# Keeping the split projection weights of a hybrid streaming encoder in HBM between blocks of rows

## The chip, the core and the metric

The kernel runs as one program on one core of a Trainium2 chip. The metric is device time in microseconds (us) of one execution; the time before is the median of three runs, 3382.91 us (3378.88 to 3388.88). The profile that is read below is one further execution, with the profiler on.

## The reference

Two layers work on 2048 prompt rows and 64 sample rows of width 1024. Cut to what matters here, one layer is:

```python
xn = rms(x, lp['norm_g'])                     # row norm, gain folded into the weights by the kernel
aq, ak, av, ag, bcq, bckv, bkr, bg, cq, ck, cv, cg, mq, mg = split_in(xn @ lp['w_in'])   # 1024 -> 3232
# four attention groups: A chunk band, B low-rank over the whole past, C stick-breaking, M memory
...
y = rms(heads(y, N_OUT_HEADS), lp['out_g'].reshape(N_OUT_HEADS, HEAD_DIM))
y = y.reshape(x.shape[:2] + (MIX_WIDTH,)) * jax.nn.silu(gates)
return x + y @ lp['w_out']                     # 1024 -> 1024
```

All of it is float32. A product of two float32 matrices is made of three matmuls of a rounded type: each factor is split into a high part and the rest (low part), and high x high, high x low and low x high are summed.

## The kernel before

**Tiles and blocks.** Rows are worked on in 17 tiles of 128 (16 of the prompt, one of the sample rows). Three blocks hold 6, 6 and 5 tiles; the sample tile is the last of the third. For each layer and block there is an input projection job (`i` in the order string of line 1366, then layer and block) and an output projection job (`o`); `m` is the projection of the memory tokens. The string sets the order of the jobs: `i00 m00 i01 i02 o00 m10 o01 i10 i11 o02 i12 o10 o11 o12`. So each layer's w_in is used by three jobs (its blocks 0, 1, 2, in that order), and so is its w_out.

**A job.** `p_stream` (line 326) walks a job's chunks of output columns: 13 for an input projection (12 of 256 columns, one of 160), 4 of 256 for an output projection. For each chunk it walks the block's tiles, and for each tile eight slices k of 128 input rows. A tile and a slice take three matmuls, lines 402 (high x high), 403 (high x low weights) and 405 (low activations x high); the sample tile leaves out line 405, and the narrow chunk joins 402 and 403 into line 400. Weights are the moving operand, so a chunk's eight slices stay in SBUF until the block's last tile is through.

**Weights.** `weights` (line 297) is a generator that `feed` (line 337) advances by two steps per tile, one chunk ahead of the matmuls. Of a chunk it loads four `raw` tiles (two slices each, 256 KB, 4 buffers, line 314), and for each slice makes a `wh` tile (2 KB per partition, 8 buffers) that holds the high part (line 304, GpSimd, gain folded in) beside the low part (line 305, VectorE). A `wh` buffer is free again when the last tile of the chunk before has used its slice.

**Beside it.** `attention` (line 1253) is a second stream of instructions: scores (855 to 858), softmax or stick-breaking (`s`, `cc`, `r`, lines 1026 to 1113), transposes (900), the split of the probabilities (903, 136) and the product with the values (925). Its loads are `qbuf`, `qr` (one buffer), `kv` (five), `bt` (one buffer, line 1176). A main loop (line 1448) takes turns between the two streams by a target curve of matmul costs, which does not count weight splits or loads. The framework then sets each engine's own order of instructions and hands out buffers by a simulation of the engines (line 1558, `schedule_with_timeline_sim=True`). Each engine runs its instructions in that order. All DMAs are issued by SyncE (SP), one after the other: one whose operand is not ready holds up all behind it.

Of the kernel before, what the change touches and what calls it, by code (L numbers as in the profile page):

```python
# [7 lines left out]
F32 = mybir.dt.float32  # L8
F32R = mybir.dt.float32r
# [9 lines left out]
COL = {}  # L19
# [45 lines left out]
def hybrid_step(  # L65
# [8 lines left out]
    nc = tc.nc  # L74
# [12 lines left out]
    def pool(name, bufs=1, **kw):  # L87
        return ctx.enter_context(tc.tile_pool(name=name, bufs=bufs, **kw))
# [4 lines left out]
    pj = pool("pj")  # L93
# [47 lines left out]
    def dt(name, shape, dtype=F32):  # L141
        return dram.tile(shape, dtype, name=name, tag=name)
# [3 lines left out]
    D = {}  # L146

    def layer_dram(l):
        d = {}
        for b, tl in enumerate(blocks):  # L150
            d["QR", b] = dt(f"qr{l}_{b}", [3, 128, len(tl) * 128])
            for g in "ABCM":
                d["Q" + g, b] = dt(f"q{g}{l}_{b}", [2, 256, len(tl) * 128])
                d["G" + g, b] = dt(f"g{g}{l}_{b}", [128, len(tl), 256])
        for g in "ABC":
            d["KV" + g] = dt(f"kv{g}{l}", [2, NH, HD, (NT + 3) // 4, 2, 512])
        for s in ("SA", "SB", "SC", "M", "SM"):
            d["KV" + s] = dt(f"kv{s}{l}", [2, NH, HD, 2, 256])
        d["KR"] = dt(f"kr{l}", [128, NT * 128])
        d["KRS"] = dt(f"krs{l}", [128, 256])  # L160
        d["Y"] = {t: dt(f"y{l}_{t}", [128, 1024]) for t in range(NT + 1)}
        D[l] = d

# [111 lines left out]
    class Job:  # L275
# [1 line left out]


        def __init__(self, tiles, loader, norm, wsrc, gcols, chunks, need=None, start=None, side=None, second=None,
                     sample=True):  # L280
            self.tiles, self.loader, self.norm = list(tiles), loader, norm
            self.wsrc, self.gcols, self.chunks = wsrc, gcols, chunks
            self.need, self.start, self.side, self.second = need, start, side, second
            self.need_fold = sample
            self.acts = {}
            for c in chunks:
                left[c[3]] = left.get(c[3], 0) + len(self.tiles)
# [8 lines left out]

    def weights(job, c0, w, out):

        gc = job.gcols()

        def split(raw, k):
            hl = pj.tile([128, 512], F32R, tag="wh", name="wh", bufs=8)
            h, lo = hl[:, 0:w], hl[:, w:2 * w]
            G.tensor_scalar(out=h, in0=raw, scalar1=gc[:, k:k + 1], scalar2=1.0, op0=ALU.mult, op1=ALU.mult)  # L304
            V.scalar_tensor_tensor(out=lo, in0=raw, scalar=gc[:, k:k + 1],  # L305
                                   in1=h.bitcast(F32), op0=ALU.mult, op1=ALU.subtract)
            out.append((hl[:, 0:2 * w], h, lo))

        n = 2
        src = job.wsrc[:, 8 * c0:8 * (c0 + w)].rearrange("p (k c) -> p k c", k=8)  # L310
        raws = []
        for k in range(0, 8, n):
            raw = pj.tile([128, n, 256], F32, tag="raw", name="raw", bufs=4)
            nc.sync.dma_start(out=raw[:, :, 0:w], in_=src[:, k:k + n])
            raws.append(raw)
            yield 0
            if k > 0:
                for i in range(n):
                    split(raws[-2][:, i, 0:w], k - n + i)
                    yield 0  # L320
        for i in range(n):
            if i:
                yield 0
            split(raws[-1][:, i, 0:w], 8 - n + i)
# [396 lines left out]
    def load_x(l):  # L721
        def loader(t):
            def f(x, q):
                cs = slice(q * 512, (q + 1) * 512)
                if l > 0 and t == SAMP:
                    for e in range(2):
                        nc.sync.dma_start(out=x[64 * e:64 * e + 64], in_=X1[t][0:64, cs])
                elif l > 0:
                    nc.sync.dma_start(out=x, in_=X1[t][:, cs])
                elif t == SAMP:  # L730
                    for e in range(2):
                        nc.sync.dma_start(out=x[64 * e:64 * e + 64], in_=x_sample[:, cs])
                else:
                    nc.sync.dma_start(out=x, in_=x_prompt[t * 128:(t + 1) * 128, cs])
            return f
        return loader

    def in_proj(l, b):
        def side():
            yield from caches(l)  # L740
            done.add(("caches", l))

        return Job(blocks[b], load_x(l), True, w_in[l], lambda: LC[l]["gc"][:, 0:8], chunk_fns(l, b),
                   need=("out", l - 1, b) if l > 0 else None,
                   start=lambda: layer_consts(l), side=side if b == 1 else None,
                   second=lambda: layer_weights(l))

    def mem_proj(l):
        d = D[l]
# [63 lines left out]
    def out_proj(l, b):  # L813
        d = D[l]

        def loader(t):
            def f(x, q):
                cs = slice(q * 512, (q + 1) * 512)
                if t == SAMP:
                    for e in range(2):  # L820
                        nc.sync.dma_start(out=x[64 * e:64 * e + 64], in_=d["Y"][t][0:64, cs])
                else:
                    nc.sync.dma_start(out=x, in_=d["Y"][t][:, cs])
            return f

        def fin(c):
            def fn(t, pp, rstd):
                xr = pj.tile([128, 256], F32, tag="ev", name="xr", bufs=3)
                cs = slice(c * 256, (c + 1) * 256)
                if l > 0:  # L830
                    nc.sync.dma_start(out=xr, in_=X1[t][:, cs])
                elif t == SAMP:
                    G.memset(xr, 0.0)
                    nc.sync.dma_start(out=xr[0:64], in_=x_sample[:, cs])
                else:
                    nc.sync.dma_start(out=xr, in_=x_prompt[t * 128:(t + 1) * 128, cs])
                yield
                V.tensor_tensor(out=xr, in0=pp, in1=xr, op=ALU.add)
                yield
                if l < L - 1:  # L840
                    nc.sync.dma_start(out=X1[t][:, cs], in_=xr)
                elif t == SAMP:
                    nc.sync.dma_start(out=y_s[:, cs], in_=xr[0:64])
                else:
                    nc.sync.dma_start(out=y_p[t * 128:(t + 1) * 128, cs], in_=xr)
            return fn

        return Job(blocks[b], loader, False, w_out[l], lambda: LC[l]["gc"][:, 16:24],
                   [(c * 256, 256, fin(c), ("out", l, b)) for c in range(4)], need=("attn", l, b))


    def scores(ps, q, qr, i, kt, kr, c0, n):
# [509 lines left out]
    for l in range(L):  # L1362
        layer_dram(l)
# [84 lines left out]
    while gens:  # L1448
# [12 lines left out]
        c = next(gens[s], "end")  # L1461
# [109 lines left out]
```

## Time and profile before

| what | value |
|---|---|
| median of 3 runs | 3382.91 us (3378.88 to 3388.88) |
| profiled execution, its own time | 3392.03 us |
| its span, first to last instruction | 3390.2 us |
| mean granted TensorE clock | 0.985 |
| matmuls / weight loads, busy | 94% / 89% |
| VectorE / ScalarE / GpSimd, busy | 80% / 57% / 47% |
| DMA engines, share of time on the kernel's own queue | 58.3% |
| HBM read / written | 378.21 MB / 173.75 MB |

PE are the matmuls, PEld the weight loads of TensorE, DVE is VectorE, ACT ScalarE, POOL GpSimd, SPq the DMA issues of SyncE. A row "X <- Y" says that X sat idle until Y ended. The profiled execution lies 9.1 us above the median of the runs.

### The profile page before, as it was taken

The numbers are of one execution on the slowest core, as the hardware profiler recorded it, in microseconds if no ns is written. First come the engines' busy times: TensorE is split into PE (matmuls) and PEld (weight loads), VectorE is DVE, ScalarE is ACT, GpSimd is POOL, SyncE is SP. The second block draws the span as 40 slices with busy tenths as digits, with TensorE's granted clock in tenths as the row PEclk, the third lists the DMA queues.
The fourth block names the chain that finished last, engine by engine and source line by source line (L and its number), as shares of the span: only waits on it lengthen the run. The fifth ranks groups of instructions, "written<-read, shape, count | busy, mean of one in ns | idle before, by whom it ended". The sixth has DMA issues, their size and how long they took to land. (4 is left out here: it accounts for less than half of the span.)

```text
span 3390.2 us, 75857 instructions
## 1 busy us (share of the span) xinstructions
PE 3177.9 (94%) x24486; PEld 3029.8 (89%) x24486; DVE 2728.9 (80%) x7976; ACT 1939.0 (57%) x5336; POOL 1598.4 (47%) x2353
## 2 busy tenths in 40 slices
PE   8999899899999998999999899988999999999898
PEld 7899899789999988999999788978898998888898
DVE  5686777999788789887778977899878888776994
ACT  4455655567665555566556665656646566654651
POOL 4564455666344256542434635477424454112563
PEclk9999999999999998999999999999999999999999
DMA  6555776435656656565566567634455766556534
GB/s 198 168 147 165 205 203 191 131 101 155 172 155 192 194 165 166 141 191 154 145 186 193 146 177 209 194 111 118 140 142 160 207 193 192 151 149 179 153 110 147
DMA packets 576123, 558.95 MB, mean 165 GB/s; under 512 B 70960, under 2 KB 478000, under 8 KB 575728
## 3 DMA queue, kind: packets, MB, share of 16 engines
q1 hardware_dynamic: 575728, 554.10, 58.3%
q8 instruction: 196, 3.21, 0.4%
q14 instruction: 199, 1.63, 0.2%
HBM read 378.21 MB, written 173.75 MB: 163 GB/s over the span
## 5 line engine op out<-in xcount | busy, mean ns | idle before, releaser
L403 PE MATMUL pp<-wh,xh 128*128 128x256 f32 x4416 | 1268.4, 291 | 33.6 <-DVE wh L305 32.3
L402 PE MATMUL pp<-wh,xh 128*128 128x256 f32 x4416 | 1259.8, 290 | 21.9 <-ACT ev L437 14.4
L405 PE MATMUL pp<-wh,xl 128*128 128x256 f32 (+1 forms) x4416 | 1250.5, 285 | 0.6 <-DVE xl L136 0.4
L403 PEld LDWEIGHTS pp<-wh,xh 128*128 128x128 f32 x4416 | 839.9, 191 | 64.0 <-DVE wh L305 51.3
L402 PEld LDWEIGHTS pp<-wh,xh 128*128 128x128 f32 x4416 | 837.5, 191 | 39.2 <-ACT ev L437 18.5
L405 PEld LDWEIGHTS pp<-wh,xl 128*128 128x128 f32 x4416 | 845.1, 192 | 9.3 <-DVE xl L136 0.8
L304 POOL TENSOR_SCALAR wh<-raw,gc 128x256 fp32r<-128x256 f32 (+1 forms) x848 | 500.1, 604 | 301.6 <-PE pp L405 146.3
L925 PE MATMUL ot<-ph,kv 128*128 128x256 f32 (+1 forms) x3104 | 591.8, 294 | 34.3 <-DVE ph L136 18.8
L903 ACT CAST ph<-pt 128x512 fp32r<-128x512 f32 (+2 forms) x840 | 451.0, 551 | 259.6 <-PE pt L900 231.0
L136 DVE TENSOR_TENSOR ph<-pt,ph 128x512 fp32r<-128x512 f32 (+2 forms) x840 | 525.9, 634 | 68.7 <-ACT ph L903 64.8
L900 PE MATMUL pt<-identr,s 128*128 128x128 f32 x3056 | 509.7, 277 | 25.2 <-POOL s L1113 8.0
L925 PEld LDWEIGHTS ot<-ph,kv 128*128 128x128 f32 x3104 | 458.7, 191 | 56.5 <-DVE ph L136 28.0
L1113 POOL TENSOR_TENSOR s<-s,r 128x512 f32<-128x512 f32 (+3 forms) x328 | 359.6, 1102 | 311.4 <-DVE r L1110 136.9
L305 DVE SCALAR_TENSOR_TENSOR wh<-raw,gc,wh 128x256 fp32r<-128x256 f32 (+1 forms) x848 | 472.5, 582 | 25.0 <-POOL wh L304 22.9
L1110 DVE TENSOR_TENSOR_SCAN r<-cc,r 128x512 f32<-128x512 f32 (+3 forms) x328 | 406.5, 1250 | 15.9 <-ACT cc L1093 14.4
L139 POOL TENSOR_TENSOR st<-st,mhalf 128x4 f32<-128x4 f32 (+1 forms) x312 | 283.3, 913 | 270.9 <-DVE st L463 240.4
L855 PE MATMUL ps<-kv,qbuf 128*128 128x512 f32 (+3 forms) x1024 | 376.7, 371 | 25.7 <-DVE ph L136 5.4
L900 PEld LDWEIGHTS pt<-identr,s 128*128 128x128 f32 x3056 | 361.8, 141 | 43.6 <-POOL s L1113 12.4
L856 PE MATMUL ps<-kv,qbuf 128*128 128x512 f32 (+3 forms) x1024 | 351.1, 345 | 0.0
L437 ACT ACTIVATE ev<-pp,xst 128x256 f32<-128x256 f32 (+1 forms) x424 | 199.9, 473 | 161.7 <-PE pp L405 118.4
L1093 ACT ACTIVATE cc<-ps 128x512 f32<-128x512 f32 (+3 forms) x328 | 178.2, 544 | 192.5 <-DVE ps L1090 153.7
L1051 ACT ACTIVATE s<-s,nm 128x512 f32<-128x512 f32 (+3 forms) x328 | 212.6, 651 | 107.2 <-DVE nm L1043 74.3
(171 smaller groups left out, 5128.9 us busy)
## 6 DMA issues: line engine op xcount, KB each, us to landing
raw<-in_w_in SPq DMA_DIRECT2D x288, 256.0 KB, 3.5
kv<-kvC SPq DMA_DIRECT2D x128, 256.0 KB, 4.3
kv<-kvB SPq DMA_DIRECT2D x128, 256.0 KB, 4.4
kv<-kvA SPq DMA_DIRECT2D x96, 256.0 KB, 4.5
raw<-in_w_out SPq DMA_DIRECT2D x96, 256.0 KB, 3.4
y<-y SPq DMA_DIRECT2D x136, 128.0 KB, 2.5
xin<-y SPq DMA_DIRECT2D x64, 256.0 KB, 3.5
qC<-kt SPq DMA_DIRECT2D x34, 256.0 KB, 3.0
```

The source lines that it names most:

```text
L136: (eng or V).tensor_tensor(out=dst, in0=src, in1=hi.bitcast(F32), op=ALU.subtract)
L304: G.tensor_scalar(out=h, in0=raw, scalar1=gc[:, k:k + 1], scalar2=1.0, op0=ALU.mult, op1=ALU.mult)
L305: V.scalar_tensor_tensor(out=lo, in0=raw, scalar=gc[:, k:k + 1], in1=h.bitcast(F32), op0=ALU.mult, op1=ALU.subtract)
L402: T.matmul(pp, lhsT=xh[:, k], rhs=wh, start=(k == 0), stop=False)
L403: T.matmul(pp, lhsT=xh[:, k], rhs=wl, start=False, stop=end)
L405: T.matmul(pp[:, 0:w], lhsT=xl[:, k], rhs=wh, start=False, stop=(k == 7))
L855: T.matmul(ps[:, 0:w], lhsT=q[:, 0, qs], rhs=kt[:, c0:c0 + w], start=True, stop=False)
L900: T.transpose(pt[:, (u + x) * 128:(u + x + 1) * 128], self.p_of(i, j), ident)
L903: A.copy(out=ph[:, 0:w], in_=pt[:, 0:w])
L925: T.matmul(ot[:, e * lo, il[0]:il[0] + n], lhsT=p["vt"](j), rhs=phl[:, e, u * 128:(u + n) * 128], start=start and e == 0, stop=stop and e ...
L1110: V.tensor_tensor_scan(r[:, 0:w][:, ::-1], cc[:, 0:w][:, ::-1], cc[:, 0:w][:, ::-1], r[:, w:w + 1], ALU.mult, ALU.min)
L1113: G.tensor_tensor(out=s[:, 0:w], in0=s[:, 0:w], in1=r[:, 1:w + 1], op=ALU.mult)
```

## The change

Two tensors per layer are added in HBM, `WI` (128 x 16 x 3232) and `WO` (128 x 16 x 1024). The jobs of a layer's block 0 (i00, o00, i10, o10) split as before, and after each split store the whole `wh` tile. The jobs of blocks 1 and 2 (i01, i02, o01, i11, o02, i12, o11, o12) load each slice's `wh` tile from there, eight DMAs per chunk, and split nothing. `raw` and `wh` tiles now share one set of 12 buffers of 2 KB per partition, in place of 4 and 8. The memory projection (m00, m10) splits as before and stores nothing.

```diff
@@ layer_dram
+        d["WI"] = dt(f"wi{l}", [128, 16 * sum(w for _, w in COL.values())])
+        d["WO"] = dt(f"wo{l}", [128, 16 * 1024])
@@ Job.__init__
-                     sample=True):
+                     sample=True, store=None, first=True):
+            self.store, self.first = store, first
@@ weights(job, c0, w, out)
+        if job.store is not None:
+            kept = job.store[:, 16 * c0:16 * (c0 + w)].rearrange("p (k c) -> p k c", k=8)
+        if not job.first:
+            for k in range(8):
+                hl = pj.tile([128, 512], F32R, tag="wh", name="wh", bufs=12)
+                nc.sync.dma_start(out=hl[:, 0:2 * w].bitcast(F32), in_=kept[:, k])
+                out.append((hl[:, 0:2 * w], hl[:, 0:w], hl[:, w:2 * w]))
+                yield 0
+            return
         gc = job.gcols()
         def split(raw, k):
-            hl = pj.tile([128, 512], F32R, tag="wh", name="wh", bufs=8)
+            hl = pj.tile([128, 512], F32R, tag="wh", name="wh", bufs=12)
             h, lo = hl[:, 0:w], hl[:, w:2 * w]
             G.tensor_scalar(out=h, in0=raw, scalar1=gc[:, k:k + 1], scalar2=1.0, op0=ALU.mult, op1=ALU.mult)
             V.scalar_tensor_tensor(out=lo, in0=raw, scalar=gc[:, k:k + 1],
                                    in1=h.bitcast(F32), op0=ALU.mult, op1=ALU.subtract)
+            if job.store is not None:
+                nc.sync.dma_start(out=kept[:, k], in_=hl[:, 0:2 * w].bitcast(F32))
             out.append((hl[:, 0:2 * w], h, lo))
...
-            raw = pj.tile([128, n, 256], F32, tag="raw", name="raw", bufs=4)
+            raw = pj.tile([128, n, 256], F32, tag="wh", name="raw", bufs=12)
@@ in_proj
-                   second=lambda: layer_weights(l))
+                   second=lambda: layer_weights(l), store=D[l]["WI"], first=b == 0)
@@ out_proj
-                   [(c * 256, 256, fin(c), ("out", l, b)) for c in range(4)], need=("attn", l, b))
+                   [(c * 256, 256, fin(c), ("out", l, b)) for c in range(4)], need=("attn", l, b), store=d["WO"], first=b == 0)
```

Counted in the built programs: splits 848 before and 304 now, on GpSimd and on VectorE alike; `raw` loads of w_in and w_out 408 and 136; new are 272 stores and 544 loads of `wh`. DMA issues on SP are 3581 and 4125.

GpSimd in the output projection of layer 0's block 1 (o01), before: `s<-s,r` is the last product of stick-breaking, `r` its running product, `wh` the split.

```order
L1107 MEMSET r 128x1
L1113 TENSOR_TENSOR s<-s,r 128x384
L1113 TENSOR_TENSOR s<-s,r 128x512
L304 TENSOR_SCALAR wh<-raw,gc 128x256 x4
L1113 TENSOR_TENSOR s<-s,r 128x512
L304 TENSOR_SCALAR wh<-raw,gc 128x256 x4
L1113 TENSOR_TENSOR s<-s,r 128x512 x3
L1107 MEMSET r 128x1
L1113 TENSOR_TENSOR s<-s,r 128x512 x2
L1107 MEMSET r 128x1 x2
```

The same place on GpSimd in the changed program (line numbers are 14 higher there):

```order
L1121 MEMSET r 128x1
L1127 TENSOR_TENSOR s<-s,r 128x384
L1127 TENSOR_TENSOR s<-s,r 128x512 x5
L1121 MEMSET r 128x1
L1127 TENSOR_TENSOR s<-s,r 128x512 x2
L1121 MEMSET r 128x1 x2
```

The eight splits of one chunk, which stood among the five products, are gone, and the products follow each other.

SP in the input projection of layer 1's block 1 (i11), before, at the end of the chunk `cv` (its last results go out to `o_cvp`): `raw` is a weight load, `bt`, `qbuf` and `qr` are loads of the attention, `kvC` and `qB` results of the projection.

```order
L608 DMA o_cvp<-ev 128x256
L503 DMA qB_1_182<-kt 128x4x128
L1153 DMA qbuf_89<-qA_0_171 64x2x256
L1154 DMA qbuf_89<-qA_0_171 64x256
L1176 DMA bt<-in_bias_p 128x640
L314 DMA raw<-in_w_in 128x512
L1153 DMA qbuf_87<-qM_0_177 64x2x256
L1154 DMA qbuf_87<-qM_0_177 64x256
L522 DMA kvC_199<-vs 64x4x128 x2
L314 DMA raw<-in_w_in 128x512
```

The same place on SP in the changed program, where `wh<-wi` are loads of stored slices:

```order
L622 DMA o_cvp<-ev 128x256
L307 DMA wh<-wi_209 128x512 x4
L527 DMA qr_1_181<-qrs 128x2x128
L517 DMA qB_1_184<-kt 128x4x128
L1190 DMA bt<-in_bias_p 128x640
L1167 DMA qbuf_89<-qA_0_173 64x2x256
L1168 DMA qbuf_89<-qA_0_173 64x256
L536 DMA kvC_201<-vs 64x4x128 x2
L527 DMA qr_1_181<-qrs 128x2x128
L528 DMA qr_1_181<-qrs 128x128
L517 DMA qB_1_184<-kt 128x4x128
L307 DMA wh<-wi_209 128x512 x2
```

Single `raw` loads, spread among the others, have become groups of two to four `wh` loads, and the loads of `bt` and `qbuf` stand behind a group of four.

## Rows read from the trace of the kernel before

**Rows 1.** The page's first part: engine, busy us, share of span, instructions.

```profile
PE 3177.9 (94%) x24486; PEld 3029.8 (89%) x24486; DVE 2728.9 (80%) x7976; ACT 1939.0 (57%) x5336; POOL 1598.4 (47%) x2353
```

**Rows 2.** Stretches of single jobs: start:end length, busy PE PEld DVE ACT POOL, clock, DMA.

```profile
362.00:817.00 455.00, 419.14 (x3246) 397.93 (x3245) 384.26 (x1070) 279.14 (x768) 260.49 (x365) 0.99 0.59 163
817.00:1152.00 335.00, 328.68 (x2584) 317.35 (x2583) 269.61 (x904) 200.66 (x563) 144.02 (x236) 1.00 0.63 175
...
1333.00:1480.00 147.00, 142.63 (x1098) 135.37 (x1098) 123.95 (x237) 84.18 (x192) 71.12 (x93) 0.99 0.61 167
1480.00:1906.00 426.00, 416.50 (x3281) 402.19 (x3279) 343.72 (x1169) 255.18 (x751) 180.25 (x289) 1.00 0.60 166
1906.00:2446.00 540.00, 488.62 (x3667) 461.15 (x3668) 458.62 (x1262) 334.71 (x923) 293.65 (x401) 0.97 0.57 159
2446.00:2570.00 124.00, 123.66 (x955) 118.17 (x955) 93.33 (x301) 65.03 (x185) 23.54 (x44) 1.00 0.52 142
2570.00:2940.00 370.00, 350.65 (x2732) 334.00 (x2732) 300.84 (x1100) 230.30 (x690) 168.93 (x263) 1.00 0.64 181
...
3141.00:3317.00 176.00, 160.84 (x1215) 151.08 (x1215) 163.46 (x284) 97.95 (x215) 103.92 (x123) 0.98 0.49 136
3317.00:3390.00 73.00, 61.07 (x474) 58.95 (x472) 29.29 (x62) 6.39 (x13) 19.59 (x34) 0.94 0.47 144
```

**Rows 3.** The page's groups by line: count, busy us, mean ns, idle before.

```profile
L304 POOL TENSOR_SCALAR wh<-raw,gc 128x256 fp32r<-128x256 f32 (+1 forms) x848 | 500.1, 604 | 301.6 <-PE pp L405 146.3
...
L305 DVE SCALAR_TENSOR_TENSOR wh<-raw,gc,wh 128x256 fp32r<-128x256 f32 (+1 forms) x848 | 472.5, 582 | 25.0 <-POOL wh L304 22.9
```

**Rows 4.** Waits of TensorE's weight loads: idle us, times, longest us.

```profile
PEld pp L403 <- DVE wh L305: 51.3, 85, 2.3
...
PEld pp L402 <- POOL wh L304: 6.0, 9, 1.7
```

**Rows 5.** Timeline of TensorE at the start of 2711 us: start, length.

```profile
2711.08 0.28 PE L405 MATMUL pp<-wh,xl 128*128 128x256 f32 x1
2711.20 0.29 PE L402 MATMUL pp<-wh,xh 128*128 128x256 f32 x1
2711.32 0.28 PE L403 MATMUL pp<-wh,xh 128*128 128x256 f32 x1
```

**Rows 6.** Timeline of SP, four `raw` loads issued in a row: start, length.

```profile
2712.41 2.03 SPq L314 DMA_DIRECT2D raw<-in_w_in  x4
```

**Rows 7.** Line 314 from 2712 to 2714.6 us: issue (ns), and time to landing.

```profile
L314 SPq DMA_DIRECT2D raw<-in_w_in x4: 376/386/588, 2712.4 to 2714.1; - x4
...
DMA to landing us min/median/max: 3.0/4.2/6.1
```

**Rows 8.** Line 314 over the whole span: issue (ns, min/median/max), and time to landing.

```profile
L314 SPq DMA_DIRECT2D raw<-in_w_in x312: 322/384/1842, 3.5 to 2879.5; - x156
...
DMA to landing us min/median/max: 2.3/3.4/8.3
```

**Rows 9.** The page's DMA queue: packets, MB, share of 16 engines' time.

```profile
q1 hardware_dynamic: 575728, 554.10, 58.3%
```

**Rows 10.** Waits for single loads, on TensorE and VectorE: idle us, times, longest.

```profile
PE ptx L259 <- DMA xin<-in_x_prompt: 11.9, 6, 6.5
PE ps L858 <- DMA qr<-qr: 10.0, 12, 1.8
...
PE ptx L259 <- DMA xin<-y: 6.3, 5, 1.8
...
PE ptx L259 <- DMA xin<-x: 3.5, 3, 2.4
...
DVE s L980 <- DMA bt<-in_bias_p: 21.5, 10, 5.5
```

**Rows 11.** The split's instructions over the span: ns, min/median/max.

```profile
L304 POOL TENSOR_SCALAR wh<-raw,gc x848: 392/595/1487, 7.6 to 3372.1; 128x256 fp32r<-128x256 f32 x159, 128x160 fp32r<-128x160 f32 x11
L305 DVE SCALAR_TENSOR_TENSOR wh<-raw,gc,wh x848: 351/484/1408, 8.1 to 3373.0; 128x256 fp32r<-128x256 f32 x159, 128x160 fp32r<-128x160 f32 x11
```

## Prediction

> **What bounds the kernel now.** I read the page's engine line first, then busy time by job, then who TensorE waits for, then the loads. The reader is to see four things.
>
> TensorE is the engine to beat: its matmuls are busy 3178 of 3390 us, VectorE 80%, GpSimd 47% [rows 1]. Whatever the change takes from VectorE and GpSimd is worth at most the 212 us in which no matmul ran.
>
> That idle time is not even. The rows by job cover, in order, i01, i02, o01, i10, i11, o02, i12, o11 and o12 (the stretches run from a job's first projection matmul to its last, to a microsecond or two) [rows 2]. Length less PE gives the idle time: i01 35.9, i02 6.3, o01 4.4, i10 9.5, i11 51.4, o02 0.3, i12 19.4, o11 15.2, o12 11.9 us. The three worst per microsecond beside o12 are those where VectorE is fullest: i01 84%, i11 85%, o11 93%. Where it is 75 to 81% (i02, i10, o02, i12), idle time is 35.5 of 1255 us, 2.8%. One row speaks against a simple rule: o01 has VectorE at 84% and idles 3%.
>
> The split itself is waited for: 57.3 us of idle weight loads, in 94 waits [rows 4]. It comes late because a `wh` buffer is free only when the last tile has passed; GpSimd sits 146 us waiting for that, its later work behind it [rows 3].
>
> The loads are latency more than bandwidth: one 256 KB `raw` load lands 3.4 us after issue in the median, 8.3 at worst [rows 8], and the DMA engines are busy 58.3% [rows 9].
>
> **The change part by part.** The sum is made against the profiled execution, 3392 us, which lies 9 us above the median of the runs; 9 us are taken off at the end.
>
> *Splits removed.* 848 − 304 = 544 go. At the means of 582 and 604 ns [rows 3] that is 317 us of VectorE and 329 us of GpSimd. None of it is time of the kernel by itself; it counts as far as TensorE waits. There are two ways.
>
> (a) Direct waits. 57.3 us over 848 splits, of which 544 go: 57.3 × 544/848 = 37 us. That assumes later blocks wait as the first ones do. Bounds: 0 (the load is waited for in the same place, counted in c) and 57 (all waits lie in the later blocks). I take −37.
>
> (b) Relief of VectorE. i01 and i11 lose 104 splits each, 60.5 us, o11 32, 18.6 us. VectorE's share falls to 71% (324 of 455), 74% (398 of 540) and 82% (145 of 176), the band in which the other jobs idle 2.8%. At that rate the three would idle 33 us of 1171 in place of 102: −69, in which their part of (a), 37 × 240/544 = 16, is counted already, so −53. The o01 row shows that a full VectorE need not mean idle matmuls, and these jobs differ in their mix of attention as well. Bounds 0 and −53; between the two I take half, −27. The other later jobs sit at low idle now, and I give them nothing more than (a).
>
> *Loads added.* 8 loads in each of 68 chunks (4 × 13 + 4 × 4), 544 in all, in place of 272 `raw` loads; with the stores, 544 more issues on SP at 0.384 us [rows 8], 209 us of a queue that spans 3390. Four of a chunk's eight slices find a free buffer a chunk ahead, behind nothing. The other four need the buffers of the chunk that ends, and this is the new wait.
>
> (c) From the release of a buffer (last tile, slice 0) to the matmul that needs its successor (next chunk, first tile, slice 4) stand 7 + 4 slices of three matmuls at 0.118 us [rows 5]: 11 × 0.354 = 3.9 us, and for the fourth slice, counted from that first release, 14 × 0.354 = 5.0 us. That is without attention between; projection matmuls are 13520 of 24486, so on average the time is 7.1 and 9.0 us. The load: the nearest row is a group of four `raw` loads of the same size, in the middle of a busy job. The last was issued 1.7 us after the first and landed at most 6.1 us later, so 7.8 us after the first issue [rows 6, 7]. So the fourth slice is up to 2.8 us late where nothing lies between, and 1.2 us early on average. Bounds: 0, and 68 × 2.8 = 190 us. I take 2.8 for the four changes of chunk into and within o12, which has no attention beside it, and 0.2 for the other 64, because the average is covered and the thin ones are few: 11 + 13 = +24.
>
> (d) Traffic. A wide slice is 256 KB, a narrow one 160: stores 69.7 MB, loads 139.5, less 69.7 of `raw`: +139.5 MB on 554.1. At the cost per byte of now the queue's 58.3% [rows 9] become 73%. What cannot be issued early pays: `qr` and `bt` with one buffer, and `xin`. TensorE's idle time behind `qr` and `xin` is 31.7 us [rows 10]. A third more is +10. Bounds 0, and 60 if `bt`, which stops VectorE by up to 5.5 us at a time [rows 10], grows with it.
>
> (e) Stores. 272 in the first blocks, each behind its split on SP, then 0.384 us of issue: 104 us of SP in jobs where it also carries all else. A `wh` tile is read for a whole chunk anyway, so the store's reading holds no buffer. Cover: SP is ahead of its consumers. If that is gone, every late load there costs. Bounds 0 and 20; I take +3.
>
> *Shared buffers.* 12 in place of 8 + 4: in first blocks a chunk needs 8 + 4 as before, so nothing. If `raw` tiles took places that splits want, the waits of [rows 4] in the first blocks, 57 − 37 = 20 us, would grow; I leave it at 0, with ±5.
>
> Sum: −37 − 27 + 24 + 10 + 3 = −27. 3392 − 27 = 3365, less 9: **3356 us**, 0.8% faster.
>
> **The rivals.** *A, the bursts (slower).* In the changed order the loads stand in groups, of the buffers of an ending chunk up to eight in a row, 2 MB, and the same single queue carries `bt`, `qbuf` and `qr` right behind a group of four. A group of four kept its last load 7.8 us where a lone one takes 3.4 [rows 6, 8]. If at each of 68 chunk changes a load of the attention or of the weights holds TensorE 1.0 us beyond what (c) and (d) have, that is +68: 3424 us. It decides from 0.4 us per change on (27 us). For it: SP holds everything behind an unready load, and two of the five rows of [rows 10], loads with one or two buffers, have waits over 5 us. Against it: `kv` has five buffers and `qbuf` three, and most slack is over a burst's length.
> The Trainium skill, DMA: Bandwidth & Descriptors, "Latency and other measured facts", gives HBM access 0.2 us on average and 2 us at high load. No row before separates the two; 2 us at 68 changes would be 136 us, an estimate from that page alone.
>
> *B, the wait only moves (no change).* Matmuls wait for loads at chunk changes as they did for splits: (c) at 0.75 us per change is 51 in place of 24, and the sum is 0: 3383. For it: landing, 3.4 us, and the thinnest cover, 3.9, are close. Against it: half of a chunk's slices come a chunk ahead, where no split did.
>
> *C, a larger gain.* The splits hold VectorE and GpSimd longer than their work: 351 ns at least but 582 in the mean, 392 and 604 [rows 3, 11]. Something stretches them by some 220 ns; if it is the two engines in each other's way, then the instructions that remain get shorter as well, and waits behind `ph` and `r` shrink everywhere. Idle time of the eight later jobs is 145 us in [rows 2]; two thirds of it gone, with (c) to (e) at half, is −97 + 18 = −79: 3304 us.
> The Trainium skill, SBUF — State Buffer, "Who interferes with whom", says that a VectorE instruction with two SBUF inputs contends with a GpSimd instruction that reads SBUF. The line 305 split has two such inputs, and its spread of 351 to 1408 ns agrees with that rule; by it C holds in full, without it the spread has another cause and only (a) and (b) remain.
>
> That the change does not do what it says is excluded: the counts in the built program are 304 splits and 544 loads.
>
> **How the numbers follow.** Forecast 0.50, A 0.22, B 0.15, C 0.13. What a measurement here can tell from no change is about 0.3%, 10 us: below 3373 is faster, above 3393 slower. The forecast's own range is 3325 to 3380; a tenth of it falls within 10 us of no change. Faster: 0.45 + 0.13 + a little of B = 0.61. Same: 0.05 + 0.11 = 0.16. Slower: 0.22 of A and a touch of B = 0.23. The range reaches down into C and up into A: 3295 to 3415.
>
> **What would show it.** VectorE's busy time near 2729 − 317 = 2412 us and GpSimd's near 1270, both lower still if C holds. The queue near 73% and 694 MB. Waits of `pp` on the split near 20 us, and a new row, `pp` on the load of `wh`, near 24: 50 is B. Idle time in i01, i11 and o11, found by the same jobs, down from 102 to about 60. Rows of waits on `qr`, `xin` and `bt` a third higher; doubled is A, as is SP waiting long for `pp` with attention loads behind it. Wrong is the forecast if VectorE falls as said and the three jobs idle as before: then VectorE was not what TensorE waited for, and (b) fails.

## The result: 3432.6 us, 1.4% slower

The changed kernel takes 3432.61 us in the median of 4 runs (3414.83 to 3440.45), the kernel before 3381.88 beside it on the same chip: 1.0143 times as long, 95% interval 1.0118 to 1.0168. The forecast was 3356, range 3295 to 3415. The profiled execution of after took 3425.42 us (span 3423.6), that of before 3392.03. One execution in all that follows, of the change with late stores, ran at a granted clock of 0.844 where every other had 0.958 or more, and is left out of the times. The first view is the engine line and the queue of after.

```profile
PE 3180.4 (93%) x24486; PEld 3032.1 (89%) x24486; DVE 2459.7 (72%) x7432; ACT 1940.3 (57%) x5336; POOL 1263.1 (37%) x1809
...
q1 hardware_dynamic: 652016, 693.60, 69.4%
```

The change does what it says: VectorE is relieved of 269 us, GpSimd of 335, the queue carries 139.5 MB more [rows 1, 9]. Relief of 600 us of engine time did not shorten the kernel. Busy time by job shows where the time went; the columns are start:end, length, busy PE, PEld, DVE, ACT, POOL, clock, DMA share, GB/s. In order: i00, i01, i02, o00, i10, i11, o02, i12, o10, o11 (o01 and o12, left out, keep their lengths to 1 us).

```profile
0.00:350.00 350.00, 321.12 (x2465) 308.88 (x2466) 235.91 (x642) 170.07 (x468) 182.04 (x315) 0.97 0.79 241
370.00:825.00 455.00, 421.49 (x3238) 403.44 (x3238) 335.50 (x965) 281.66 (x767) 201.19 (x263) 0.97 0.66 191
825.00:1175.00 350.00, 333.39 (x2577) 318.64 (x2576) 223.32 (x801) 199.39 (x561) 87.08 (x137) 1.00 0.73 206
1175.00:1324.00 149.00, 134.09 (x1045) 129.69 (x1044) 116.06 (x340) 77.23 (x208) 65.37 (x83) 0.97 0.72 222
...
1505.00:1953.00 448.00, 427.08 (x3305) 405.58 (x3304) 344.89 (x1176) 257.32 (x764) 175.31 (x285) 1.00 0.74 219
1953.00:2473.00 520.00, 477.19 (x3650) 453.39 (x3649) 400.38 (x1147) 331.01 (x914) 223.87 (x291) 0.98 0.66 190
2473.00:2603.00 130.00, 126.00 (x952) 119.76 (x951) 78.64 (x264) 63.35 (x181) 5.48 (x11) 0.99 0.59 170
2603.00:2979.00 376.00, 347.76 (x2693) 331.49 (x2694) 255.83 (x999) 229.70 (x685) 109.55 (x161) 0.99 0.74 210
2994.00:3189.00 195.00, 178.04 (x1354) 166.84 (x1353) 148.51 (x492) 103.74 (x283) 41.40 (x58) 0.99 0.71 208
3189.00:3351.00 162.00, 152.47 (x1193) 146.06 (x1192) 138.56 (x239) 97.58 (x212) 75.19 (x85) 0.99 0.60 169
...
```

The same view of before for the first-block jobs that the rows ahead of the prediction lack (i00, o00, o10):

```profile
0.00:343.00 343.00, 317.65 (x2466) 306.32 (x2467) 235.64 (x639) 170.42 (x468) 185.38 (x315) 0.98 0.60 168
1152.00:1287.00 135.00, 128.24 (x1027) 124.06 (x1027) 112.58 (x328) 72.93 (x198) 63.15 (x83) 0.99 0.60 178
2954.00:3141.00 187.00, 174.19 (x1326) 164.37 (x1327) 141.25 (x470) 100.15 (x271) 39.47 (x55) 0.98 0.60 164
```

Beside [rows 2], the reader is to see two groups. The four first-block jobs, which split as before (from shared buffers) and store as well, are longer: i00 343 to 350, o00 135 to 149, i10 426 to 448, o10 187 to 195, together 51 us. The eight later jobs together are 8 us shorter: i11 540 to 520 and o11 176 to 162 gain, i02 335 to 350, i12 370 to 376 and o02 124 to 130 lose. The loss has the size of what happens in jobs that the prediction gave 3 us.

Two limits of this view. The two profiled executions lie 33 us apart, not 51 as the medians do: that of before is 9 us above its median, that of after 7 below. And each length is from one execution: in a kernel that differs from before by four small stores (section 3 of the experiments) they moved by up to 6 us, so a few us in one job say nothing.

The waits of after follow (idle us, times, longest us), first TensorE's weight loads, then GpSimd and SP; the last row is SP in before.

```profile
PEld pp L416 <- DMA wh<-wi: 35.6, 47, 3.4
...
PEld pp L417 <- DVE wh L317: 11.6, 18, 2.0
...
PEld pp L416 <- POOL wh L316: 8.7, 8, 3.2
...
PEld pp L416 <- DMA wh<-wo: 7.2, 11, 1.7
```

```profile
POOL wh L316 <- DMA raw<-in_w_in: 65.5, 27, 8.3
...
POOL wh L316 <- DMA raw<-in_w_out: 44.0, 10, 11.9
```

```profile
SPq L320 <- DVE wh L317: 42.1, 54, 4.0
```

```profile
SPq L314 <- DVE wh L305: 154.5, 146, 13.4
```

Waits for splits fell from 57.3 to 20.3 us [rows 4], the 20 of the forecast. Waits for the new loads are 42.8 us by the same measure, where the forecast had 24. Of the matmuls' waits, those for `qr` and for `xin` from `y` went up by a third, 10.0 to 13.6 and 6.3 to 8.2 us; with `xin` from the prompt and from `x`, which fell, the four rows of [rows 10] went from 31.7 to 34.9. GpSimd waits 110 us for `raw`, in before 7.0 us for that of w_in. SP stands 42 us at a store until its split is done, with all loads queued behind it. That SP stands at splits is not new: in before it stood 154.5 us at `raw` loads, whose buffer a split had to free.

### The profile page after: what moved, and what is told of

It is laid out like the page before. It is cut to its first block, busy times and chain, and to the rows that moved or that the text cites. A ratio compares the mean times of both kernels' runs of the same rounds, so it can differ in the third digit from the quotient of the medians.

```text
span 3423.6 us, 75123 instructions
## 1 busy us (share of the span) xinstructions
PE 3180.4 (93%) x24486; PEld 3032.1 (89%) x24486; DVE 2459.7 (72%) x7432; ACT 1940.3 (57%) x5336; POOL 1263.1 (37%) x1809
## 3 DMA queue, kind: packets, MB, share of 16 engines
q1 hardware_dynamic: 652016, 693.60, 69.4%
## 5 line engine op out<-in xcount | busy, mean ns | idle before, releaser
L316 POOL TENSOR_SCALAR wh<-raw,gc 128x256 fp32r<-128x256 f32 (+1 forms) x304 | 164.7, 552 | 283.8 <-PE pp L419 74.0
L869 PEld LDWEIGHTS ps<-kv,qbuf 128*128 128x128 f32 x1024 | 196.3, 192 | 61.9 <-issue 11.6
```

What stands on the lines that cost most here:

```text
L869: T.matmul(ps[:, 0:w], lhsT=q[:, 0, qs], rhs=kt[:, c0:c0 + w], start=True, stop=False)
```

## The experiments

Times are medians; a ratio is to runs of the kernel before on the same chip, whose medians lay between 3379.7 and 3384.3 us; the cost is the difference of the two medians.

**1. Which part costs.** Three kernels, each the kernel before with one or two parts of the change, and one that is the change with one part undone.

```diff
# e1_shared_only: one set of buffers, nothing else
-            raw = pj.tile([128, n, 256], F32, tag="raw", name="raw", bufs=4)
+            raw = pj.tile([128, n, 256], F32, tag="wh", name="raw", bufs=12)
# e2_stores_only: every block splits; first blocks store too
+            if job.store is not None:
+                nc.sync.dma_start(out=kept[:, k], in_=hl[:, 0:2 * w].bitcast(F32))
# e3_shared_and_stores: both.  e4_separate_8_and_4: the whole change, but
-            raw = pj.tile([128, n, 256], F32, tag="wh", name="raw", bufs=12)
+            raw = pj.tile([128, n, 256], F32, tag="raw", name="raw", bufs=4)   # and wh: bufs=8
```

> The kernel before, with raw and wh tiles in one set of 12 buffers; nothing is stored, nothing loaded from a store. Theory R (raw loads come late, since a raw tile must take its turn among the wh tiles): all 848 splits are hit, so 20 to 60 us slower than before, and GpSimd waits over 100 us in total for DMA raw (7 us before). Theory T (traffic of the stores in first blocks): same as before within 10 us. Theory A (bursts of loads at chunk changes): same as before within 10 us.

> The kernel before, its buffers of 4 and 8 unchanged, plus the 272 stores of the first blocks; all blocks still split. Theory R: within 10 us of before. Theory T: 25 to 50 us slower, in i00, o00, i10 and o10. Theory A: within 10 us of before.

> The changed kernel without its loads: shared 12 buffers and stores in first blocks, all blocks split. The step from here to the changed kernel is what loading in place of splitting does. Theory R: slower than before by about as much as the shared buffers alone, and slower than the changed kernel by up to 40 us, since all blocks pay for late raw tiles. Theory T: 25 to 50 us slower than before, about as the changed kernel. Theory A: within 10 us of before, and the changed kernel loses its 50 us only against this one.

> The changed kernel with raw (4) and wh (8) in sets of their own: raw tiles come a chunk ahead as before, but a later block has no spare wh buffer, so all eight slices of a chunk are loaded at its start. Theory R: first blocks as long as before the change (i10 about 425 us in place of 448), later blocks lose, since slice 0 to 3 now come at the chunk change too: cover 11 k-steps becomes 7, 2.5 us, against 3.4 us of landing, 1 to 3 us at each of 68 changes, so 3440 to 3600 in all. Theory T: first blocks stay as long as in the changed kernel. Theory A: later blocks lose most, 60 us or more beyond the changed kernel.

| kernel | time, us | ratio (95% interval) | cost, us |
|---|---|---|---|
| e1, shared buffers alone | 3409.0 | 1.0082 (1.0056 to 1.0107) | 26 |
| e2, stores alone | 3430.85 | 1.0140 (1.0118 to 1.0162) | 47 |
| e3, both | 3436.16 | 1.0143 (1.0121 to 1.0165) | 53 |
| e4, the change with 8 and 4 buffers | 3467.96 | 1.0241 (1.0217 to 1.0265) | 85 |

So the 272 stores alone cost 47 us, nearly all of the loss, and loads in place of splits, the change less "both", are worth 0 within the error. Shared buffers cost 26 us alone, and 5 beside the stores, which is within the error. The wait behind them, first of the run with shared buffers, then of before:

```profile
POOL wh L304 <- DMA raw<-in_w_in: 148.8, 75, 7.9
```

```profile
POOL wh L304 <- DMA raw<-in_w_in: 7.0, 2, 4.1
```

A `raw` load now takes its turn behind split slices for a buffer, and comes late. With 4 and 8 apart the later blocks' loads find only 8 places, and waits for them rise from the 42.8 us above to 86; the shared 12 serve the loads and harm the splits.

The stores alone, in their jobs (i00, o00, i10, o10):

```profile
0.00:349.00 349.00, 319.09 (x2465) 304.29 (x2466) 236.76 (x637) 169.73 (x468) 187.07 (x313) 0.99 0.79 241
1163.00:1311.00 148.00, 134.41 (x1042) 129.03 (x1041) 115.18 (x337) 77.72 (x208) 64.45 (x83) 0.97 0.72 223
1507.00:1956.00 449.00, 423.30 (x3294) 405.73 (x3293) 343.79 (x1173) 258.22 (x760) 179.11 (x290) 0.99 0.73 218
3000.00:3190.00 190.00, 172.90 (x1328) 162.11 (x1327) 143.24 (x477) 100.81 (x276) 39.82 (x55) 1.00 0.69 204
```

These are the lengths of after to 1 us but for o10. SP's waits for splits over this whole run, at `raw` loads and at stores:

```profile
SPq L328 <- DVE wh L317: 95.9, 96, 4.8
SPq L320 <- DVE wh L317: 55.8, 83, 13.4
```

Together they are 152 us, no more than the 154.5 of before: the stores do not add to this standing, they move part of it from `raw` loads to themselves. Nor does the loss follow it. In i10 the row at stores is 24.8 us with stores alone, 12.0 in after and 11.2 in the run with held order of section 3; i10 is 23, 22 and 48 us longer than before.

**2. What of a store costs: its wait, its bytes, its issue.** All but the last from stores alone (e2).

```diff
# e5_late_stores: issued in the chunk's third tile
+                    if i == 2 and j.store is not None and j.first:
+                        nc.sync.dma_start(out=kept[:, k], in_=whl.bitcast(F32))
# e6_tiny_stores
+                nc.sync.dma_start(out=kept[:, k, 0:32], in_=hl[:, 0:32].bitcast(F32))
# e7_stores_that_do_not_wait: from a constant tile
+                nc.sync.dma_start(out=kept[:, k], in_=job.lc()["wkh"][:, 0:2 * w].bitcast(F32))
# e8_late_stores_both_sets: the whole change, stores as e5, and for a later block's loads
+                if job.turn[0] % 3 == 2:
+                    hl = pj.tile([128, 2, 256], F32, tag="raw", name="raw", bufs=4)   # else wh, bufs=8
```

> The kernel before with the 272 stores alone (every block still splits; 8 and 4 buffers as before), each store issued while the chunk's third tile is projected, when its split has long been done, in place of right behind the split. Three theories of the 47 us that the stores alone cost: H, a store waits on SP for its split and holds up the loads queued behind it; T, the 69.7 MB take DMA time from the loads; I, 272 more issues (104 us of SP) are too many wherever they stand. H: 3380 to 3398 us, SP's waits for a split gone. T: 3415 to 3435. I: 3415 to 3435.

> The kernel before with the 272 stores right behind their splits, but each stores only 32 of a slice's columns (16 KB; the rest is not stored, and every block still splits). Waits and issues are those of the run with whole stores (3430.85 us), bytes are 4.4 MB in place of 69.7. H (head of line): 3415 to 3435. T (traffic): 3380 to 3395. I (issues): 3415 to 3435.

> The kernel before with whole stores at the same places in the program, but their data come from a constant tile that is there since the layer's start, so no store waits for a split (what is stored is not the split; some 16 stores before that tile exists are left out; every block still splits). H: 3380 to 3398. T: 3415 to 3435. I: 3415 to 3435.

> The whole change, with two edits: stores late (third tile of the chunk), and raw and split slices in their own 4 and 8 buffers as before, where a later block's loads take two of three from the set of 8 and one of three from the set of 4. H: the stores cost under 10, and the raw loads of first blocks stand as before; what remains is relief less the waits for loads, 3370 to 3400. T or I: the stores still cost 40, 3410 to 3440.

| kernel | time, us | ratio (95% interval) | cost, us |
|---|---|---|---|
| e5, late stores | 3420.44 | 1.0117 (1.0097 to 1.0138) | 41 |
| e6, small stores | 3400.77 | 1.0066 (1.0047 to 1.0084) | 21 |
| e7, stores from a constant | 3482.32 | 1.0300 (1.0278 to 1.0322) | 103 |
| e8, the change with late stores | 3429.09 | 1.0147 (1.0124 to 1.0170) | 49 |

H, the head of line alone, falls: stores whose waits at SP were halved (105 to 53 us over all stores, by the sums of SP's waits at that line) still cost 41. The small stores did not do only what was expected of them. The 32 columns that they read belong to the high part, so they wait for GpSimd's half of a split and no longer for VectorE's:

```profile
SPq L320 <- POOL wh L316: 50.9, 97, 4.0
```

Their waits at SP are 54 us in all, half of 105 as well. So the 26 us between whole and small stores are bytes and shorter waits together. Late and small stores have the same waits, 53 and 54 us, and lie 20 us apart; by that pair, which also differs in the place of the stores, the bytes are about 20 of the 47 us.

The stores without a wait miss their purpose: the framework's order let them run ahead in bursts (a fortieth of the span at 338 GB/s), i00 and i02 lost 51 and 45 us, and i10, from which the stores had gone, took 428, as before.

**3. Is it the order?** Adding an instruction lets the framework order all engines anew. With the stores of e2, 2585 of VectorE's 7976 places have another instruction than before, by the two traces. Three kernels hold the other instructions in the order of before (e10 not the `raw` loads of first blocks, e11 no `raw` load); one was to perturb it with nothing in it to cost time.

```diff
# e9 (as e2), e10 (as e8, but stores right behind splits), e11 (as e1)
+                for o in order:                      # per engine, of the kernel before
+                    for x, y in zip(o, o[1:]):
+                        tc.add_manual_dep(traced[y], traced[x].name, nosync, reason="order of before")
# e12_four_small_stores: as e6, and
+            if job.store is not None and c0 == 0 and k == 0:
```

> The kernel before with the 272 stores right behind their splits, as in the run with stores alone (3430.85 us), but every other instruction is held, on each of the five engines, in the order in which the kernel before has it; only the stores are put between them. Theory O: the stores cost because the simulation that orders the instructions takes another order for all engines once they are there, and by themselves cost little: 3380 to 3400. Theory S: the stores themselves cost, by their 69.7 MB and by SP's waits for splits, whatever the order: 3420 to 3440. Between, 3400 to 3420, is a share of each.

> The whole change (stores, loads in the later blocks, no splits there), with what is left of the kernel before held in its order on every engine but for the raw loads of first blocks; raw and split slices in their own 4 and 8 buffers, a later block's loads taking two of three from the 8 and one of three from the 4. O: the gain from splits that are gone shows, less the waits for loads: 3345 to 3380. S: the stores still cost their 40: 3400 to 3435.

> The kernel before with raw and split slices in one set of 12 buffers and nothing else (3409.0 us in the earlier run), every instruction but the raw loads held in the order of the kernel before. O: 3378 to 3392. Rival: raw loads and splits take turns on the buffers, so that a raw load waits for one that is released late, whatever the order: 3400 to 3415.

> The kernel before with four stores of 16 KB in all (the first slice of the first chunk of each first block, 32 columns; every block splits). There is nothing in it to cost a microsecond but the order, which the simulation sets anew. O: the time moves by 8 us or more in either direction, and jobs without any store differ by several us each. S: 3380 to 3388, and no job differs by more than 2 us.

| kernel | time, us | ratio (95% interval) | cost, us |
|---|---|---|---|
| e9, stores, order held | 3509.79 | 1.0385 (1.0360 to 1.0409) | 129 |
| e10, whole change, order held | 3580.53 | 1.0598 (1.0573 to 1.0623) | 199 |
| e11, shared buffers, order held | 3434.79 | 1.0170 (1.0145 to 1.0194) | 54 |
| e12, four small stores | 3382.02 | 1.0008 (0.9996 to 1.0021) | 1 |

Theory O falls three times: with the order of before the same stores cost 129 us, not 47, shared buffers 54, not 26, and the whole change 199. The new order is the remedy, not the ill: it takes back more than half. The fourth kernel says less. Its time does not move, i00 is 6 us shorter, i12 4, the rest within 3; but its four stores changed only 34 of VectorE's 7976 places, so it hardly perturbed the order. With the order held the loss is where the stores are, i00, o00, i10, o10 (36, 14, 48 and 18 us longer than before):

```profile
0.00:379.00 379.00, 326.88 (x2462) 314.23 (x2463) 234.75 (x638) 168.72 (x468) 184.29 (x314) 0.95 0.73 222
1191.00:1340.00 149.00, 130.72 (x1022) 126.01 (x1021) 111.08 (x327) 72.88 (x198) 62.42 (x81) 0.94 0.70 216
1537.00:2011.00 474.00, 431.37 (x3275) 414.23 (x3273) 344.21 (x1167) 254.91 (x752) 179.72 (x288) 0.96 0.69 206
3047.00:3252.00 205.00, 180.87 (x1319) 170.97 (x1320) 141.56 (x469) 100.20 (x272) 37.53 (x54) 0.93 0.64 185
```

**4. The same question with the order held, and the loads by themselves.**

```diff
# e13: e9 with 32 columns per store.  e14: e9 with a chunk's stores behind the next chunk's raw loads
+        with tc.issue_after(x.ins):                  # x: a raw load; late[:2]: two stores
+            for out, in_ in late[:n]:
+                nc.sync.dma_start(out=out, in_=in_)
# e15: both.  e16: e8 without its stores but those of chunk 0, which every chunk then loads
+            if job.store is not None and c0 == 0:
+                nc.sync.dma_start(out=kept[:, k], in_=hl.bitcast(F32))
```

> As the run with stores and held order (3509.8 us, 129 above before; its first-block jobs hold 116 of that), but each store carries 16 KB in place of 256 or 160 (32 columns; the rest is not stored). Waits and issues stay. B (the bytes cost): 3383 to 3405. W (SP stands at a store until its split is done, and all loads behind it stand too) or Q (272 issues at 0.384 us are 104 us of SP): 3475 to 3515.

> Held order and whole stores, but a chunk's stores are issued behind the raw loads of the next chunk, two behind each (those loads wait for the same splits already in the kernel before). Bytes and issues stay, SP's waits for a split go. W: 3383 to 3415. B or Q: 3475 to 3515.

> Both edits: 16 KB per store, and issued behind the next chunk's raw loads, order held. Only the 272 issues are left. Q: 3470 to 3510. W or B: 3383 to 3400.

> The loads of the later blocks in place of their splits, with 32 stores in all: a later block loads its eight slices, in the right size, from those of the first chunk (so it computes with the wrong weights). Raw and split slices in their own 4 and 8 buffers, loads two to one from both; order free. The forecast's terms a to d, -37 - 27 + 24 + 10: 3350 us. Rival, after the run with late stores and both sets (10 us above the one with late stores alone): the loads gain nothing or lose a little: 3383 to 3398.

| kernel | time, us | ratio (95% interval) | cost, us |
|---|---|---|---|
| e13, small stores | 3468.66 | 1.0250 (1.0227 to 1.0273) | 84 |
| e14, stores behind loads | 3506.41 | 1.0363 (1.0341 to 1.0385) | 122 |
| e15, small stores behind loads | 3437.69 | 1.0167 (1.0146 to 1.0187) | 53 |
| e16, loads without stores | 3394.32 | 1.0032 (1.0019 to 1.0044) | 10 |

No theory holds alone. Taking the bytes away is worth 44 us at the split and 69 behind the loads, shorter waits again included: over all stores SP waits 99 us in e9 and 69 in e13, 91 in e14 and 65 in e15. What stays of small stores, 53 to 84 us, is issue, wait, or both: 272 issues at 0.382 us, the median of that line in e15, are 104 us of SP. The edit of e14 failed in its aim. SP's waits at stores, here of the run with held order and of the one behind loads, are alike, so those `raw` loads went out before some of the splits were done:

```profile
SPq L324 <- DVE wh L321: 36.6, 74, 3.5
```

```profile
SPq L309 <- DVE wh L329: 34.6, 58, 3.5
```

So the wait was never taken away without something else, and its share stays open.

The run of loads alone measures the forecast's terms a to d (with 4 and 8 buffers apart, both used for loads), and gives +10 us (+6 to +15) where −30 stood. TensorE's weight loads wait 22.5 us for splits there and 45.5 for the new loads: the 57.3 us of before are not saved but exchanged. Its rows for i02, i11, i12 and o11:

```profile
810.00:1163.00 353.00, 334.84 (x2574) 319.76 (x2573) 224.90 (x803) 199.55 (x561) 85.91 (x135) 0.99 0.73 204
...
1918.00:2447.00 529.00, 483.49 (x3650) 458.33 (x3648) 400.60 (x1152) 332.57 (x917) 221.35 (x294) 0.97 0.65 187
...
2575.00:2975.00 400.00, 367.42 (x2799) 350.62 (x2800) 269.16 (x1045) 241.47 (x717) 112.35 (x167) 0.97 0.73 209
3160.00:3326.00 166.00, 156.56 (x1217) 149.25 (x1216) 145.97 (x252) 101.03 (x219) 79.56 (x91) 0.99 0.57 165
```

i11 and o11, where VectorE was fullest, gain 11 and 10 us against [rows 2] (i11 8, counted from its first matmul, 2 us behind the start of its row there), i01 and o01 2 and 4. i02 takes 353 in place of 335, and i12, from its first matmul to that of the next job, 400 in place of 384:

```profile
2570.00:2954.00 384.00, 362.13 (x2800) 342.99 (x2800) 312.06 (x1141) 239.39 (x718) 169.64 (x264) 1.00 0.65 182
```

In these two jobs TensorE's matmuls sit idle 12 and 11 us longer; the rest is longer matmul time. In i12 they wait 11.2 us for the new loads (in `wh` and in `raw` buffers), and `qr` and `xin` cost about what they did before:

```profile
PE pp L421 <- DMA wh<-wi: 8.6, 8, 3.6
...
PE pp L421 <- DMA raw<-wi: 2.6, 3, 1.4
```

In i02 they wait 5.7 us for the new loads, and more for `qr` and `xin` (4.3 and 3.9 us; 0.4 and 1.8 in before), which SP issues behind loads of `wh` that wait 19.3 us until the last tile frees a buffer:

```profile
SPq L312 <- PE pp L422: 19.3, 22, 3.7
```

```profile
PE ps L877 <- DMA qr<-qr: 4.3, 3, 2.6
PE ptx L261 <- DMA xin<-y: 3.9, 2, 3.6
```

Both jobs have five tiles per chunk where block 1 has six; but i01, with six, waits 6.6 us for its loads too, so why i12 waits most is not shown.

**5. Off SP's queue, and the part that gains.**

```diff
# e17_stores_from_scalar_queue: e2 with
+                nc.scalar.dma_start(out=kept[:, k], in_=hl[:, 0:2 * w].bitcast(F32))
# e18: i10 and o10 store (by ScalarE), i11 and o11 load, all others split
+                   ... store=D[l]["WI"] if l == 1 and b < 2 else None, first=l == 0 or b != 1)
```

> The kernel before with the 272 whole stores right behind their splits, issued by ScalarE in place of SP, order free (the same from SP: 3430.9 us, +47). Every block splits. If SP's queue is what costs (its issue time and its standing at splits): 3385 to 3408, the bytes being left. If the bytes cost most of it: 3415 to 3435. If ScalarE, now standing at splits with softmax work behind it, costs as much as SP did: 3425 to 3460.

> The change where the run without stores showed a gain from it: only i11 and o11 load, only i10 and o10 store (136 stores, issued by ScalarE), all other jobs split; raw and split slices in their own 4 and 8 buffers, loads two to one from both. By that run i11 gives 8 and o11 10 us; the stores of i10 and o10 cost about 23 from SP (i10 427 to 449, o10 187 to 190), less from ScalarE. If they cost under 10: 3370 to 3380, below both kernels. If they cost as from SP: 3385 to 3395.

| kernel | time, us | ratio (95% interval) | cost, us |
|---|---|---|---|
| e17, stores from ScalarE's queue | 3424.97 | 1.0130 (1.0116 to 1.0144) | 43 |
| e18, layer 1, block 1 | 3390.96 | 1.0027 (1.0015 to 1.0038) | 9 |

Issued by ScalarE the stores cost 43 us, where the ranges of the second and the third case meet; which of the two it is, the time can't tell. SP is rid of them, but ScalarE's own work sits behind the issues, most of all the split of the probabilities and the eviction:

```profile
L320 ACTq DMA_DIRECT2D wi<-wh x208: 326/327/1682, 8.9 to 1919.8; - x104
...
  ACT ph L917: 25.8, 5
  ACT ev L451: 23.6, 6
```

The last kernel shows its gain (i11 521, o11 171 us) and its price (i10 446, o10 197, each to the next job's first matmul): together 9 us slower than before, the best of the versions that store whole slices, with half of the stores, and still behind the kernel before.

## Why the prediction was wrong

**The step that failed is (e).** It gave the 272 stores 3 us, with "Cover: SP is ahead of its consumers" and 20 us as the upper bound; alone they cost 47. No row stood behind the cover. SP's timeline of before, in i10 (start, length of the issue, what), has a stretch without it:

```profile
1507.20 1.19 SPq L1122 DMA_DIRECT2D kv<-kvB  x2
1508.49 0.53 SPq L314 DMA_DIRECT2D raw<-in_w_in  x1
1509.12 0.37 SPq L536 DMA_DIRECT2D kr<-krt  x1
1509.58 0.61 SPq L1153 DMA_DIRECT2D qbuf<-qB  x1
1510.30 1.93 SPq L1158 DMA_DIRECT2D qr<-qr  x4
```

From 1507.20 to 1512.23 issues fill 4.63 of 5.03 us; a store that is put in there moves every load behind it. That is one stretch: over all of i10, SP's single issues fill 58% in before and 69% with the stores alone. The step also left the bytes of the stores to (d), which spread them over the kernel; they fall into four jobs, whose DMA share goes from 0.60 to between 0.69 and 0.79. What the runs show in place of (e): 47 us, all in the storing jobs, of which 20 to 26 go when the bytes go (the larger figure with shorter waits at SP in it). The rest hangs on the place on SP, issue and wait, not told apart. By which waits it reaches TensorE is not shown: in i10 its idle time goes from 9.5 to 25.7 us with stores alone, and no single wait has more than 3 of it.

(e) is about half of the miss. It is 44 us too small, and (a) to (d) promised −30 where the run of loads alone has +10; the forecast missed by 77.

**(a), (b), (c).** (a) is right in its rows: 37 us fewer waits for splits. (c) is too small, 43 for 24, and in the wrong place: it gave o12 11 us and i12 3, where 4.3 and 14.3 were measured. What the splits no longer cost, the loads do. (b) moved as said and was too large. Its own sign was idle time in i01, i11 and o11, down from 102 to about 60; it is 86 in after and 89 in the run of loads alone, though VectorE's share fell, in after to 74, 77 and 86%, where the forecast had 71, 74 and 82. By length, i01, i11, o01 and o11 together gain 25 to 27 us in the run of loads alone, against the 34 that (a) to (d) make there (27 of b, 18.5 of a, less 6 of c and 5 of d). What failed most beside (e) is "The other later jobs sit at low idle now": i02, o02, i12 and o12 were to lose 4 us by the same sum and lose 40 (18, 4, 16 and 2). VectorE's relief shows no gain where it was not full, and these jobs pay the loads.

**(d)** was 10 us on 31.7. The four rows rise by 3 us in after and by 9 in the run of loads alone; the queue is at 69.4% for 73. It is not what failed.

**Shared buffers**, 0 ± 5, are 26 us alone. "A chunk needs 8 + 4 as before" counted places and not turns. Beside the stores they add only 5.

**The rivals.** A came out on the side and within 9 us of the time, by luck and not by its mechanism. It wanted 1.0 us at each of 68 chunk changes beyond (c) and (d). The run of loads alone has 21 us of waits beyond (c) and none beyond (d), 0.3 us per change, below the 0.4 from which A decides; the loss that makes the result is in jobs that load nothing. B is right in its mechanism, 43 us of waits for loads where it had 51 (45.5 in the run of loads alone), and lacked the stores. C is excluded. GpSimd's busy share fell from 47 to 37%, and the splits that remain take 568 ns in the mean, 582 before [rows 3]; the split of the probabilities, VectorE's costliest row, takes 635 ns, 634 before; VectorE fell by 269 us, less than the 317 of the forecast. The Trainium skill, SBUF — State Buffer, "Who interferes with whom", names a contention of the two engines; no run here shows that fewer GpSimd instructions make VectorE's shorter.

The Trainium skill, DMA: Bandwidth & Descriptors, "Issuing engines are not separate DMA queues", says that DMAs of any engine run on the same 16 DMA engines, and that issuing from several saves only the sequencer's time, which is usually small beside the DMA. The run from ScalarE's queue agrees: the DMA share in i10 is 0.74, 0.73 from SP, and 4 us of 47 came back, though ScalarE's own work pays there too. One issue is small beside its DMA here as well, 0.38 us beside 1.8 to 2.6 us from issue to landing for the small stores with held order; but 272 of them on one queue, with their waits, cost 0.2 to 0.3 us each.

What stays open: how the 21 us of small stores with the order free, and the 53 to 84 with it held, divide between SP's issue time and its standing at splits; and through which waits the stores reach TensorE.

## What to carry to other kernels

Before an edit adds a DMA to a queue, read the issuing engine's own timeline in the jobs concerned: SP issued in 58% of i10 and in nine tenths of one stretch of it, and a DMA that waits for a producer holds up all loads behind it. Taking work from an engine paid where that engine was fullest (i11, o11), not by its total. Storing once to save two recomputations did not pay here, because the jobs that store had no room for it on that queue and in the DMA engines, and the jobs that load waited for the loads as they had for the splits. And when a store is made smaller to take its bytes away, see which instruction it then waits for.

## What the runs showed of the hardware

In one place a gap cost more than its length. In i10 of the run with held order and whole stores, TensorE stood 5.37 us, and from 1747 to 1752 us the granted clock was 0.50, the lower of its two levels, 1.2 GHz, while matmuls ran without a gap.

```profile
1746.16 0.48 PE L873 MATMUL ps<-kv,qbuf 128*128 128x128 f32 x1 [5.37 <-ACT bqr L700]
```

```profile
1742.00:1747.00 5.00, 0.83 (x4) 0.84 (x5) 2.47 (x10) 2.65 (x9) 2.72 (x5) 0.88 0.64 180
1747.00:1752.00 5.00, 5.00 (x25) 5.00 (x25) 4.29 (x19) 3.89 (x15) 2.07 (x4) 0.50 0.55 157
```

Of the 48 us that i10 lost there, 15 are longer matmul time (416.5 to 431.4 us busy, clock 1.00 to 0.96), not idle time. Over the whole of that run matmuls are busy 26 us longer than in before (3203.9 for 3177.9), of 111 that it lost.
